# Second block's attention in a two-block network: keys, queries and values reordered, softmax in batches of four heads

## The chip, the cores and the metric

The kernel runs on one core of a Trainium2 chip. The metric is the device time of one execution in microseconds (us). The core has a matrix engine (TensorE, PE in the profile, its weight loads PEld), VectorE (DVE), ScalarE (ACT), GpSimd (POOL), and SyncE (SP), whose queue issues the loads.

## The reference, cut to what matters

256 tokens of width 1024 go through two blocks. The first has a recurrent branch, an attention and a layer of retrieved experts (PEER). The second has two layers; each is a feed-forward half step, a mixer and a second feed-forward half step. The mixer of the second block's first layer is a convolution; that of its second layer is the attention this document is about:

```
k, v = split(rms_norm(x, g_kv) @ w_kv)          # 8 heads of 128
q    = rms_norm(x, g_pre) @ w_q * 128 ** -0.5
s    = q . k - slope[h] * (t_query - t_key)     # causal; slope[h] = 2 ** -(h + 1)
y    = softmax(s) . v
x    = x + rms_norm(y @ w_o, g_post)
```

The keys and values come from one normalisation of x, the queries from another. All 256 tokens lie in one block of the attention, so that no block is left out.

## The kernel before, in words

Products of activations and weights are made in three parts (`mm3`, lines 155 to 159): each operand is split into a high part and the rest, and high x high, high x rest and rest x high are summed in PSUM. Weights come from HBM in units: `Stream.units` (line 115) issues one load of 1 MB into a raw buffer (line 125), ScalarE copies the high part (line 138), VectorE takes the difference (line 141). One load gives two units. In the second block there are three raw buffers and eight buffers for split units (`st.pools`, line 909).

There are two forms of a product. `gemm_rows` (line 230) makes rows of tokens: the tokens' transposed activations are the stationary operand, weights of 512 columns move, and its `tail` says how many of the contraction's chunks are left for tokens 128 to 255 to the end; with `tail=8` all products of tokens 0 to 127 come first, and `late()` makes the others. `gemm_i` (line 216) makes transposed results: the weights are stationary, and the activations of all 256 tokens move at once.

A normalisation is made for 128 tokens at a time. `Pre` (line 950) takes the sum of squares on ScalarE (line 170), the mean on VectorE (line 178), the power on POOL (line 180), scales the rows on VectorE (line 213), transposes them four at a time on TensorE (line 194), copies the high part on ScalarE (line 162) and takes the difference on VectorE (line 163). The feed-forward function `ffn` (line 959) ends with `post(1, ...)` for tokens 128 to 255, and hands the last transpositions on as `pend`, which `run(pend)` at line 1331 issues.

The attention (lines 1335 to 1384) goes in this order:

- values, by `gemm_rows` with `tail=8` (lines 1348 to 1353), evicted by ScalarE into `vr`;
- keys (line 1354), then queries (line 1355), by `gemm_i`, evicted by ScalarE into `kT` and `qT`;
- a loop over eight heads and two halves of the tokens (lines 1359 to 1381): the scores on TensorE (1363), the alibi added (1367) and the maximum (1368) on VectorE, the exponential with its sum on ScalarE (1370), the reciprocal on VectorE (1371), one or two transpositions (1374) with a copy by VectorE (1376), the products with the values (1380), and a scaled eviction by ScalarE (1381);
- the transpositions of the output rows (line 1384), and the output product by `gemm_rows` (line 1385).

Large work tiles of the second block (`Q`, line 918) share five buffers. PSUM has two banks under `pm`, two under `pt` and four under `pa` (line 86).

The engines' queues are not in the written order: the framework's scheduler takes, for each engine, the instruction that comes first in the written order among those that it holds to be ready, with a model of its own for the times. `after` (line 149) adds an order by hand; nothing around the change has one.

Of the kernel before, what the change touches and what calls it, by code (L numbers as in the profile page):

```python
# [9 lines left out]
F32 = mybir.dt.float32  # L10
# [4 lines left out]
AF = mybir.ActivationFunctionType  # L15
ALU = mybir.AluOpType
AX = mybir.AxisListType
# [4 lines left out]
T = 256  # L22
# [44 lines left out]
def _body(nc, tc, ctx, a, out, dbg):  # L67
# [17 lines left out]
    def ps(tag):  # L85
        return pp.tile([128, 512], F32, name=tag, tag=tag, bufs={"pm": 2, "pt": 2, "pa": 4}[tag])
# [173 lines left out]
    def rows_src(w, n):  # L260
        v = w.rearrange("(n c p) d -> n p c d", c=2, p=128)
        return [v[i] for i in range(n)]
# [3 lines left out]

    # ------------------------------------------------------------------ block 1
    with ExitStack() as s1:
# [58 lines left out]

        # recurrent branch input and causal conv
        xp = S([128, 8, TT + 3], F32, "xp")
# [13 lines left out]

        # latent projections
        def small_pair(k, n):
# [56 lines left out]

        # log_sigmoid(lambda) * 8
        lam = pv[:, P_LAM, :]
# [16 lines left out]

        # recurrent gates
        gw, gt = [], []
# [39 lines left out]

        # keys, values, queries
        kT, kodd, vv, qr, qT = [], [], [], [], []
# [88 lines left out]

        # recurrent output
        yT = (S([128, 8, T], F32R, "yTh"), S([128, 8, T], F32R, "yTl"))
# [5 lines left out]

        # attention, with other products between the heads
        mask = tmp("mask", [128, 144 + TT], 1)
# [128 lines left out]

    # ------------------------------------------------------------------ PEER
    with ExitStack() as s2:
# [209 lines left out]

    # ------------------------------------------------------------------ block 2
    with ExitStack() as s3:
# [7 lines left out]
        def t256(name):  # L915
            return bp.tile([128, 256], F32, name=name, tag="t256", bufs=7)
# [158 lines left out]

        # conv mixer
        cv = Q([128, 8, T], F32, "cv")
        # pieces of the convolution: chunk 0 and the first taps of 5 on Pool, two lanes (chunk, first tap, end) on
        # Vector, chunks 6, 7 and the last taps of 5 on PE; a chunk of several pieces is summed by PE, by rows
        VL = (((1, 0, 31), (3, 0, 31)), ((2, 0, 31), (4, 0, 31), (5, KQ, KQ + KS)))  # L1080
# [38 lines left out]
        def taps(lane):  # L1119
            # the sums stay in PSUM: the second read port is left to Pool  # L1120
            bank = ps("pa")
            for j, (b, k0, k1) in enumerate(lane):
                if k0 == k1:
                    return
                dst = t256("part") if k0 else cv[:, b, :]
                parts.setdefault(b, []).append(dst)
                acc = bank[:, j % 2 * T:j % 2 * T + T]
                for k in range(k0, k1):
                    u, o, w = uslot(b)[:, k:k + T], dst if k == k1 - 1 else acc, pv[:, P_DW + k, b:b + 1]
                    if k > k0:  # L1130
                        nc.vector.scalar_tensor_tensor(out=o, in0=u, scalar=w, in1=acc, op0=ALU.mult, op1=ALU.add)
                    elif k == 0:
                        nc.vector.tensor_scalar(o, u, w, pv[:, P_DB, b:b + 1], ALU.mult, ALU.add)
                    else:
                        nc.vector.tensor_scalar(o, u, w, None, ALU.mult)
                    yield

        def taps_pool(b, slot, n):
            # even and odd taps apart, four products at a time
            u = uslot(b)  # L1140
# [51 lines left out]
        def stats(b):  # L1192
            # to rows, as soon as a chunk is done
            n = len(order)
# [26 lines left out]

        # the first chunks by rows, so that the first 128 tokens start before the others are normalized
        wb = {}
# [110 lines left out]

        # block attention
        def G8(n):
# [6 lines left out]
        def ev_copy(dst, scale):  # L1343
            def fn(b, p):
                nc.scalar.activation(dst[:, b, :], p, AF.Copy, scale=scale)
            return fn

        acc, late = gemm_rows(xkv, rows_src(a["wv"], 4), 8)
        for t in range(2):
            for half in range(2):  # L1350
                nc.scalar.activation(vr[:, t, half * 512:half * 512 + 512], acc[t][half], AF.Copy)
            if t == 0:
                late()
        gemm_i([a["wk"][i] for i in range(4)], xkv, ev_copy(kT, 1.0), T)
        gemm_i([a["wq"][i] for i in range(4)], xq, ev_copy(qT, 128.0 ** -0.5), T)
        al = tmp("alibi", [128, 384], 1)
        nc.sync.dma_start(al, a["alibi"])
        orow = Q([128, 2, D], F32, "orow2")
        for h in range(8):
            for t in range(2):  # L1360
                nk = 128 * (t + 1)
                sp = ps("pm")
                nc.tensor.matmul(sp[:, :nk], qT[:, h, t * 128:(t + 1) * 128], kT[:, h, :nk], start=True, stop=True)
                sc = t256("sc2")
                mxv = small.tile([128, 1], F32, name="mxv", tag="mxv", bufs=4)
                av = al[:, 0:128] if t == 0 else al[:, 128:384]
                nc.vector.scalar_tensor_tensor(out=sc[:, :nk], in0=av, scalar=2.0 ** -(h + 1), in1=sp[:, :nk], op0=ALU.mult, op1=ALU.add)
                nc.vector.tensor_reduce(mxv, sc[:, :nk], AX.X, ALU.max, negate=True)
                rsum = small.tile([128, 1], F32, name="rsum", tag="rsum", bufs=4)
                nc.scalar.activation(sc[:, :nk], sc[:, :nk], AF.Exp, bias=mxv, accum_out=rsum)  # L1370
                nc.vector.reciprocal(rsum, rsum)
                pt = ps("pt")
                for j in range(t + 1):
                    nc.tensor.transpose(pt[:, j * 128:(j + 1) * 128], sc[:, j * 128:(j + 1) * 128], ident)
                pT = tmp("pT2", [128, 2, 128], 3)
                nc.vector.tensor_copy(pT[:, :t + 1, :], pt[:, :nk].rearrange("p (j t) -> p j t", j=t + 1))
                po = ps("pa")
                hs = slice(h * 128, h * 128 + 128)
                for j in range(t + 1):
                    nc.tensor.matmul(po[:, :128], pT[:, j, :], vr[:, j, hs], start=j == 0, stop=j == t)  # L1380
                nc.scalar.activation(orow[:, t, hs], po[:, :128], AF.Copy, scale=rsum)
        oT = (q_tile(), q_tile())
        for t in range(2):
            transposes(orow[:, t, :], 8, to_pair(oT[0], oT[1], t * 128, 128))
        acc, late = gemm_rows(oT, rows_src(a["wo"], 4), 8)
        gpost = gain(G_MPOST + 1, bp, bufs=3)
# [101 lines left out]
```

## Time and profile before

| | us |
|---|---|
| median of three runs | 2145.33 |
| lowest and highest | 2144.96, 2150.92 |
| span of the profiled execution | 2144.5 |
| TensorE busy in it | 2093.2 (98%) |
| VectorE, ScalarE, GpSimd busy | 1395.0 (65%), 1143.7 (53%), 113.6 (5%) |

The profile is one execution. A row of the timeline gives the start, the duration, the engine, the line of the code, the operation, output and input tiles, the shape and how many instructions are merged, and in brackets how long the engine had been idle before and for whom it waited. Times are from the start of the span. Matmuls overlap: the record of one lasts longer than the distance to the next start. A row of the windows gives, for a stretch of time, the busy time of each engine with the number of instructions, the granted clock of TensorE (1.00 is full) and the load of the DMA engines.

### The profile page before, as it was taken

To read this page: it belongs to the slowest core of one execution; us is meant where nothing else is said; L and a number is where in the kernel's file an instruction comes from. 1 tells how busy PE (TensorE), PEld (TensorE's weight loads), DVE (VectorE), ACT (ScalarE), POOL (GpSimd) and SP (SyncE) were. 2 spreads that over 40 slices of the span, in tenths; PEclk is the share of its full clock that TensorE was granted. 3 is DMA by queue.
4 is the path that set the end of the run, shared out by engine and by line. 5 is a ranking of instruction groups with operands and counts; after the bars stand their busy time and mean duration, and the time that the engine had idled before them with its cause. 6 is when DMAs were issued, how large, how long until landed. Compare 5 with 4: busy or idle time off the path is not lost.

```text
span 2144.5 us, 31162 instructions
## 1 busy us (share of the span) xinstructions
PE 2093.2 (98%) x12401; PEld 1838.8 (86%) x12401; DVE 1395.0 (65%) x2361; ACT 1143.7 (53%) x1903; POOL 113.6 (5%) x112
## 2 busy tenths in 40 slices
PE   8989999999999999999999999999999999999998
PEld 7889989999999988888887887887887888887886
DVE  6685668888888865555557555967556554756554
ACT  5875444576657744444446444665445444555443
POOL 2010000000000000000000000840000000000000
PEclk9999999999999999999999999999999999999999
DMA  6432554544443445555576554316554654634551
GB/s 212 160 124 96 175 175 163 185 154 159 171 162 137 147 167 191 183 195 184 189 261 230 190 184 170 118 40 248 193 180 170 217 179 157 225 120 165 188 183 72
DMA packets 65361, 365.57 MB, mean 170 GB/s; under 512 B 6704, under 2 KB 8880, under 8 KB 33472
## 3 DMA queue, kind: packets, MB, share of 16 engines
q1 hardware_dynamic: 65216, 363.59, 49.1%
q8 instruction: 97, 1.59, 0.3%
q14 instruction: 48, 0.39, 0.1%
HBM read 360.29 MB, written 2.10 MB: 169 GB/s over the span
## 4 chain that ended last, share of the span: by engine, by line
PE 87%; DVE 5%; ACT 4%; DMA 2%; issue 1%; POOL 1%; SPq 0%; POOLq 0%; DVEq 0%; ACTq 0%
PE pa L157 18%; PE pa L159 18%; PE pa L158 18%; PE pm L157 8%; PE pm L159 8%; PE pm L158 8%; PE pm L801 3%; DVE ws L141 2%; PE pt L194 2%; PE pm L1106 1%; ACT ws L138 1%; DMA raw<-in_ffn_dram 1%; POOL rr L180 1%; ACT sq L170 1%; PE pm L590 1%
## 5 line engine op out<-in xcount | busy, mean ns | idle before, releaser
L141 DVE TENSOR_TENSOR ws<-raw,ws 128x1024 fp32r<-128x1024 f32 (+1 forms) x653 | 795.7, 1225 | 519.8 <-ACT ws L138 514.9
L138 ACT ACTIVATE ws<-raw 128x1024 fp32r<-128x1024 f32 (+1 forms) x657 | 689.3, 1057 | 548.2 <-PE pa L159 347.2
L157 PE MATMUL pa<-xT,ws 128*128 128x256 f32 x1280 | 365.0, 286 | 0.0
L159 PE MATMUL pa<-xT,ws 128*128 128x256 f32 x1280 | 360.9, 282 | 0.0
L158 PE MATMUL pa<-xT,ws 128*128 128x256 f32 x1280 | 360.8, 282 | 0.0
L157 PE MATMUL pm<-ws,xT 128*128 128x512 f32 (+1 forms) x768 | 298.9, 389 | 2.3 <-ACT xT L162 2.3
L159 PE MATMUL pm<-ws,xT 128*128 128x512 f32 (+1 forms) x768 | 294.7, 384 | 2.3 <-DVE xT L163 2.2
L158 PE MATMUL pm<-ws,xT 128*128 128x512 f32 (+1 forms) x768 | 293.8, 383 | 1.1 <-DVE ws L141 1.0
L157 PEld LDWEIGHTS pa<-xT,ws 128*128 128x128 f32 x1280 | 242.1, 189 | 0.3 <-ACT xT L162 0.3
L158 PEld LDWEIGHTS pa<-xT,ws 128*128 128x128 f32 x1280 | 242.0, 189 | 0.0
L159 PEld LDWEIGHTS pa<-xT,ws 128*128 128x128 f32 x1280 | 241.9, 189 | 0.0
L157 PE MATMUL pa<-ws,ch 128*128 128x512 f32 x512 | 201.3, 395 | 1.0 <-ACT ch L162 1.0
L158 PE MATMUL pa<-ws,ch 128*128 128x512 f32 x512 | 201.9, 395 | 0.0
L159 PE MATMUL pa<-ws,ch 128*128 128x512 f32 x512 | 201.5, 394 | 0.0
L159 PEld LDWEIGHTS pm<-ws,xT 128*128 128x128 f32 x768 | 144.8, 189 | 33.0 <-DVE xT L163 3.5
L157 PEld LDWEIGHTS pm<-ws,xT 128*128 128x128 f32 x768 | 144.9, 189 | 30.3 <-ACT xT L162 4.0
L158 PEld LDWEIGHTS pm<-ws,xT 128*128 128x128 f32 x768 | 144.8, 189 | 29.9 <-DVE ws L141 2.5
L157 PE MATMUL pa<-ws,hT 128*128 128x512 f32 x352 | 141.9, 403 | 0.6 <-ACT hT L162 0.5
L159 PE MATMUL pa<-ws,hT 128*128 128x512 f32 x352 | 137.9, 394 | 0.2
L158 PE MATMUL pa<-ws,hT 128*128 128x512 f32 x352 | 137.7, 391 | 0.0
L180 POOL TENSOR_TENSOR rr<-rs,mhalf 128x1 f32<-128x1 f32 (+1 forms) x36 | 28.7, 798 | 1938.9 <-DVE rs L178 1938.9
L157 PEld LDWEIGHTS pa<-ws,ch 128*128 128x128 f32 x512 | 96.4, 188 | 23.6 <-ACT ch L162 1.2
(390 smaller groups left out, 3202.1 us busy)
## 6 DMA issues: line engine op xcount, KB each, us to landing
raw<-in_ffn_dram SPq DMA_DIRECT2D x132, 1024.0 KB, 4.9
raw<-in_peer_u_dram SPq DMA_DIRECT2D x64, 1024.0 KB, 4.9
raw<-in_peer_v_dram SPq DMA_DIRECT2D x64, 1024.0 KB, 4.9
raw<-in_win_dram SPq DMA_DIRECT2D x16, 1024.0 KB, 4.8
gain<-in_gains_dram SPq DMA_DIRECT2D x17, 512.0 KB, 5.6
raw<-in_wpq_dram SPq DMA_DIRECT2D x8, 1024.0 KB, 5.0
raw<-in_wcin_dram SPq DMA_DIRECT2D x8, 1024.0 KB, 4.9
raw<-in_wrnn_dram SPq DMA_DIRECT2D x4, 1024.0 KB, 4.9
```

The lines of the kernel that those rows point to most:

```text
L138: i = nc.scalar.activation(hi, r, AF.Copy)
L141: self.last = (eng or nc.vector).tensor_tensor(out=lo, in0=r, in1=hi.bitcast(F32), op=ALU.subtract)
L157: nc.tensor.matmul(o, wh, xh, start=first, stop=False)
L158: nc.tensor.matmul(o, wh, xl, start=False, stop=False)
L159: nc.tensor.matmul(o, wl, xh, start=False, stop=last)
L170: nc.scalar.activation(sq[:rows, :p.shape[-1]], p, AF.Square, accum_out=ss[:rows, i:i + 1])
L180: nc.gpsimd.tensor_tensor(out=r2[:rows], in0=r[:rows], in1=mhalf[:rows], op=ALU.pow)
L194: nc.tensor.transpose(p[:, j * rows:(j + 1) * rows], src[:rows, (b + j) * 128:(b + j + 1) * 128], ident[:rows, :rows])
L590: nc.tensor.matmul(sp[:, :nk], qT[h // 8][:, h % 8, t * 128:(t + 1) * 128], kT[h // 8][:, h % 8, :nk], start=True, stop=True)
L801: nc.tensor.matmul(p[:, k * 128:(k + 1) * 128], oh[:, k, 0:128], oh[:, k, 128:256], start=True, stop=True)
L1106: in_turn(nc.tensor.matmul(p[:, :T], dg, u[:, k:k + T], start=k == 0, stop=k == 30))
```

## The change

Keys come first, then queries, then values. The softmax is made by batches of four heads and one half of the tokens (`soft2`): scores and alibi are added and the maximum taken by one VectorE instruction, for which the queries of head h are scaled by 2^(h+1) more and the exponential's scale is 2^-(h+1). `flip` transposes the softmax rows of four heads into one PSUM bank and copies the bank at once, by ScalarE for the first half of the keys, by VectorE for the second. `weigh2` makes the products with the values of four heads into one bank and scales them in one VectorE instruction. The first batch's scores come after the second of the four queries products, its transpositions after the third and fourth; the second batch's scores come before the values, its transpositions between the two halves of the values. The transpositions of the output rows of tokens 128 to 255 are written behind the start of the output product. Comments are also taken out elsewhere.

```diff
-        acc, late = gemm_rows(xkv, rows_src(a["wv"], 4), 8)
...
-        gemm_i([a["wk"][i] for i in range(4)], xkv, ev_copy(kT, 1.0), T)
-        gemm_i([a["wq"][i] for i in range(4)], xq, ev_copy(qT, 128.0 ** -0.5), T)
         al = tmp("alibi", [128, 384], 1)
         nc.sync.dma_start(al, a["alibi"])
+        neg = small.tile([128, 8], F32, name="neg")
         for h in range(8):
+            nc.vector.memset(neg[:, h:h + 1], -2.0 ** -(h + 1))
+        pT = {}
...
+        def soft2(g, t):
+            nk = 128 * (t + 1)
+            sc = (tmp("xn", [128, D], 1) if t else tmp("y", [128, 512]))[:, :4 * nk].rearrange("p (h k) -> p h k", h=4)
...
+            for j in range(4):
+                h = 4 * g + j
                 sp = ps("pm")
                 nc.tensor.matmul(sp[:, :nk], qT[:, h, t * 128:(t + 1) * 128], kT[:, h, :nk], start=True, stop=True)
...
+                nc.vector.tensor_tensor_reduce(sc[:, j, :], sp[:, :nk], av, 1.0, -3e38, ALU.add, ALU.max, mxv[:, j:j + 1])
+            nc.vector.tensor_tensor(out=mxv, in0=mxv, in1=neg[:, 4 * g:4 * g + 4], op=ALU.mult)
+            for j in range(4):
+                nc.scalar.activation(sc[:, j, :], sc[:, j, :], AF.Exp, bias=mxv[:, j:j + 1], scale=2.0 ** -(4 * g + j + 1), accum_out=rsum[:, j:j + 1])
+            nc.vector.reciprocal(rsum, rsum)
+            return sc, rsum
+
+        def flip(g, t, sc):
+            if t not in pT:
+                pT[t] = Q([128, 2048], F32, "pT2")
+            v = pT[t][:, g * 512 * (t + 1):(g + 1) * 512 * (t + 1)].rearrange("p (j h q) -> p j h q", j=t + 1, h=4)
+            for j in range(t + 1):
                 pt = ps("pt")
+                for h in range(4):
+                    nc.tensor.transpose(pt[:, h * 128:(h + 1) * 128], sc[:, h, j * 128:(j + 1) * 128], ident)
+                src = pt.rearrange("p (h q) -> p h q", h=4)
+                if j:
+                    nc.vector.tensor_copy(v[:, j], src)
+                else:
+                    nc.scalar.activation(v[:, j], src, AF.Copy)
+            return v
+
+        def weigh2(g, t, v, rsum):
+            po = ps("pm")
+            for h in range(4):
+                hs = slice((4 * g + h) * 128, (4 * g + h + 1) * 128)
                 for j in range(t + 1):
...
+                    nc.tensor.matmul(po[:, h * 128:(h + 1) * 128], v[:, j, h, :], vr[:, j, hs], start=j == 0, stop=j == t)
+            o = orow[:, t, g * 512:(g + 1) * 512].rearrange("p (h w) -> p h w", h=4)
+            nc.vector.tensor_tensor(out=o, in0=po.rearrange("p (h w) -> p h w", h=4), in1=rsum.unsqueeze(2).to_broadcast([128, 4, 128]), op=ALU.mult)
...
+        gemm_i([a["wk"][i] for i in range(4)], xkv, ev_copy(kT, 1.0), T)
+        sm, pv2 = {}, {}
+        for r in range(4):
+            gemm_i([a["wq"][r]], xq, ev_q2(r), T)
+            if r == 1:
+                for t in range(2):
+                    sm[0, t] = soft2(0, t)
+            elif r > 1:
+                pv2[0, r - 2] = flip(0, r - 2, sm[0, r - 2][0])
+        for t in range(2):
+            sm[1, t] = soft2(1, t)
+        acc, late = gemm_rows(xkv, rows_src(a["wv"], 4), 8)
+        for half in range(2):
+            nc.scalar.activation(vr[:, 0, half * 512:half * 512 + 512], acc[0][half], AF.Copy)
+        for t in range(2):
+            pv2[1, t] = flip(1, t, sm[1, t][0])
+        late()
+        orow = Q([128, 2, D], F32, "orow2")
+        for g in range(2):
+            weigh2(g, 0, pv2[g, 0], sm[g, 0][1])
+        for half in range(2):
+            nc.scalar.activation(vr[:, 1, half * 512:half * 512 + 512], acc[1][half], AF.Copy)
         oT = (q_tile(), q_tile())
...
+        for g in range(2):
+            weigh2(g, 1, pv2[g, 1], sm[g, 1][1])
+        otrans2(0)
+        acc, late = gemm_rows(oT, rows_src(a["wo"], 4), 8, fill=(0, lambda: otrans2(1)))
```

## Rows read from the trace of the kernel before

**Rows 1.** The page, part 1: TensorE's busy time, share, instructions.

```profile
PE 2093.2 (98%) x12401; PEld 1838.8 (86%) x12401; DVE 1395.0 (65%) x2361; ACT 1143.7 (53%) x1903; POOL 113.6 (5%) x112
```

**Rows 2.** Windows over the stage that is changed, all engines.

```profile
1831.44:1842.69 11.25, 10.25 (x49) 8.13 (x48) 9.78 (x17) 4.67 (x9) 1.94 (x2) 1.00 0.56 198
1842.69:1857.60 14.91, 14.91 (x72) 12.02 (x73) 8.06 (x11) 8.72 (x12) 0.00 (x0) 1.00 0.39 140
1857.60:1903.35 45.75, 45.75 (x386) 45.74 (x385) 24.01 (x20) 23.99 (x35) 0.00 (x0) 1.00 0.68 240
1903.35:1923.32 19.97, 17.98 (x114) 14.45 (x113) 16.71 (x66) 15.84 (x53) 0.00 (x0) 1.00 0.22 79
```

**Rows 3.** TensorE's timeline at the start of the values' products.

```profile
1831.44 0.39 PE L157 MATMUL pa<-ws,xT 128*128 128x512 f32 x1
1831.67 0.60 PE L194 MATMUL pt<-ident,xn 128*128 128x128 f32 x4
1832.03 0.48 PE L158 MATMUL pa<-ws,xT 128*128 128x512 f32 x1
...
1842.69 0.63 PE L194 MATMUL pt<-ident,xn 128*128 128x128 f32 x4 [1.00 <-DVE xn L213]
```

**Rows 4.** TensorE's timeline in the loop over heads.

```profile
1912.16 0.63 PE L1380 MATMUL pa<-g,pT 128*128 128x128 f32 x4
1912.62 0.38 PE L1374 MATMUL pt<-ident,sc 128*128 128x128 f32 x2
...
1917.15 0.60 PE L1363 MATMUL pm<-g,qT 128*128 128x256 f32 x2
1917.59 0.96 PE L1380 MATMUL pa<-g,pT 128*128 128x128 f32 x6
```

**Rows 5.** ScalarE's timeline while the second half is normalised.

```profile
1831.40 1.06 ACT L138 ACTIVATE ws<-raw 128x1024 fp32r<-128x1024 f32 x1
1832.35 0.60 ACT L170 ACTIVATE sq<-pa 128x512 bf16<-128x512 f32 x1
...
1843.36 1.27 ACT L162 ACTIVATE xT<-pt 128x512 fp32r<-128x512 f32 x2 [3.38 <-PE pt L194]
```

**Rows 6.** VectorE's timeline in the same stretch.

```profile
1834.16 0.15 DVE L173 TENSOR_TENSOR rs<-ss 128x1 f32<-128x1 f32 x1
...
1835.60 0.14 DVE L178 TENSOR_SCALAR rs<-rs 128x1 f32<-128x1 f32 x1
...
1838.65 2.35 DVE L141 TENSOR_TENSOR ws<-raw,ws 128x1024 fp32r<-128x1024 f32 x2
1840.92 0.15 DVE L178 TENSOR_SCALAR rs<-ss 128x1 f32<-128x1 f32 x1
...
1843.99 0.69 DVE L163 TENSOR_TENSOR xT<-pt,xT 128x512 fp32r<-128x512 f32 x1 [0.78 <-ACT xT L162]
```

**Rows 7.** Windows between block 1 and PEER, TensorE alone.

```profile
287.46:290.98 3.52, 0.01 (x1) 1.00 0.96 301
...
292.29:295.95 3.66, 3.66 (x18) 0.53 0.17 55
295.95:302.00 6.05, 6.05 (x52) 1.00 0.24 58
```

**Rows 8.** Windows at the convolution's end, TensorE alone.

```profile
1419.25:1422.80 3.55, 2.81 (x13) 0.50 0.66 270
1422.80:1425.52 2.72, 2.72 (x8) 0.50 0.00 0
```

**Rows 9.** Window over block 1's attention, all engines.

```profile
135.00:208.00 73.00, 73.00 (x565) 68.53 (x564) 41.16 (x120) 41.91 (x109) 0.00 (x0) 1.00 0.34 116
```

**Rows 10.** Groups by line and shape, 1900 to 1926: busy time, mean ns.

```profile
L1367 DVE SCALAR_TENSOR_TENSOR sc<-alibi,pm 128x256 f32<-128x256 f32 x8 | 3.3, 413 | 0.0
```

**Rows 11.** Groups by line and shape, 135 to 208, block 1's attention.

```profile
L591 DVE CUSTOM_DVE_ANT_0 sc<-pm,mask 128x272 f32<-128x272 f32 x16 | 7.0, 439 | 2.1 <-PE pm L590 1.8
```

**Rows 12.** Instructions of the alibi tile: durations, first and last start.

```profile
L1357 SPq DMA_DIRECT2D alibi<-in_alibi_dram x1: 425/425/425, 1118.9 to 1118.9; - x1
```

## What was predicted before the change was run

> **What bounds the kernel now.** I read the page first, then the windows over the stage that is changed, then TensorE's timeline at both ends of it, and last the timelines of ScalarE and VectorE. The page says that TensorE is busy for 98% of the span [rows 1], so only two things can move the time: TensorE's work, which the change leaves nearly as it is, and the moments in which TensorE has nothing to do. The windows [rows 2] cut the stage in four: the values while the second half of the tokens is still being normalised (1831.44 to 1842.69), the rest of the values (to 1857.60), keys and queries (to 1903.35), the loop over heads (to 1923.32, where the output products start). Keys and queries run without a gap. The other stretches hold all that an order of work can win or lose, so I price these.
>
> Prices of TensorE's work, from one start to the next. Keys and queries: 384 products in 45.75 us [rows 2] (the row counts two that reach in), 0.119 us each. Four transpositions take 0.36 us (1831.67 to 1832.03) [rows 3], 0.09 each. In the loop, four instructions of the product with the values take 0.46 us (1912.16 to 1912.62) and two 256-wide score instructions 0.44 us (1917.15 to 1917.59) [rows 4], so 0.115 and 0.22; a 128-wide score instruction I set at 0.115 too. A 512-wide product takes 0.23 us (1831.44 to 1831.67) [rows 3]; the values have 96 of them, 22.1 us.
>
> **Idle time in the start, before.** From 1831.44 to 1857.60 there are 26.2 us. 22.1 are the values, 2.2 are six groups of four transpositions, so 1.9 us are lost. What the reader is to see: the feed-forward stage is over at 1831.44, where the first of the values' products starts, and the transpositions of the second half's normalised tokens start only at 1842.69 [rows 3]. These 11 us are covered by the values' products for tokens 0 to 127, which need the first half alone: TensorE is busy for 10.25 of 11.25 us [rows 2].
>
> **Idle time in the loop, before.** 1903.35 to 1923.32 is 19.97 us, and two of the four groups of output transpositions come after it. Work: scores 16 x 0.115 + 16 x 0.22 = 5.4, softmax transpositions 24 x 0.09 = 2.2, products with the values 48 x 0.115 = 5.5, eight output transpositions 0.7: 13.8 us. So 6.2 us are lost there, in many small steps, because TensorE has no other products between a head's softmax steps. The busy column shows only 2.0 us of idleness (19.97 less 17.98), since a matmul's record lasts longer than the distance to the next start.
> The Trainium skill says (Perfetto Trace Analysis, Identifying the Most-Contended Engine) that matmul busy time is a poor measure, and points to the weight loads instead. By it the sum below would use 19.97 less 14.45 = 5.5 us in place of 6.2, and come to 2153.3 us; by the busy column 2.0, and 2156.8 us. The trace agrees with the rule: starts give 6.2.
>
> **The change, part by part.**
> *1. Keys first (a loss).* The keys' products are 256 wide: each takes both halves of the tokens at once. So none can start before the second half is normalised, transposed and split. I assume that the chain up to there keeps its times, because all of it, and the work that it waits behind on ScalarE and VectorE, comes before the change. The second half's transpositions then start at 1842.69; ScalarE's copy follows at 1843.36 [rows 5], VectorE's difference at 1843.99 and lasts 0.69 us [rows 6]; the keys' second product needs it, so the keys run from 1844.7. From 1831.44 that is 13.3 us, in which TensorE has four groups of transpositions (1.4 us): 11.9 us lost in place of 1.9, a loss of **10.0 us**. Lower end: the chain loses time behind other work. The second square waited behind a weight copy (1831.40 to 1832.35) [rows 5]; the scaling at 1835.60 came 1.3 us after its sum; the one at 1840.92 came after a pair of weight differences that began at 1838.65 [rows 6]. Without these some 4 us go, and the loss is 6. Upper end: 11, if the second differences come later still.
> *2. The clock (a loss).* After a hole of 3.52 us, where PEER's first products wait for block 1, the granted clock was 0.53 over 3.66 us: 18 products there against 52 in the next 6.05 us [rows 7], so 3.66 - 18 x 0.116 = 1.6 us lost, at the lower of the two levels (1.2 GHz, where 2.4 is full). In the convolution the clock stood at 0.50 over 3.55 + 2.72 us [rows 8], half of which, 3.1 us, is lost at most. Here the hole is about 9 us, longer than the first, and work resumes with transpositions as in the second, part of the low stretch passing before the keys start. I take **2.0**, ends 0.3 and 3.1.
> The Trainium skill (TensorE: Matmul & The Clock Gate, Why this matters for your kernels) advises against idle gaps between bursts, since the clock falls in them. That speaks against putting the keys first; the two stretches above agree with it.
> *3. Scores and softmax under other products (a gain).* The scores of heads 0 to 3 come after the second queries product, those of 4 to 7 ahead of the values; transpositions lie under queries and values. Block 1 does its attention so, and TensorE is busy there for 73.00 of 73.00 us [rows 9]. What stays uncovered is the end: the last values eviction, the normalised rows, ScalarE's copy of 0.6 and VectorE's 0.69 before the output products can take the first half. I leave **1.5 us** of the 6.2 there; ends 0 (block 1's row) and 6.2 (nothing won). Gain 4.7.
> *4. VectorE and ScalarE, at nothing.* The sum of score and alibi, 0.41 us for 256 columns [rows 10], and the maximum behind it become one instruction, of which block 1 shows 0.44 for 272 columns [rows 11]. Sixteen copies of softmax rows become two of 512 on VectorE and four on ScalarE, sixteen scaled evictions become four on VectorE. Both engines get less to do, and the cover is wide: over keys and queries each is busy for 24.0 of 45.75 us [rows 2]. If the cover went, one batch would show, four of 0.44 = 1.8 us on VectorE and about as much again on ScalarE. Eight memsets and the four-column multiplications are tiny and free to run early.
> *5. The queues.* SP's loads of 1 MB each are the same twelve in another order: the keys' take the place of the values' first four, loaded during the feed-forward stage. The values' units must be kept until their late half, so the output weights are split only while the last products run; this costs nothing if VectorE keeps the 1.2 us a unit of the pair at 1838.65, up to 1.5 us if not (in the ends of 3). The alibi load was issued at 1118.9 [rows 12], 780 us ahead of its use, and stays early. POOL's queue holds nothing that moves.
> *6. Buffers.* The new transposed softmax needs two of five large buffers; both halves' normalised tokens (four) and the queries hold all five until the queries are done. So the first batch's transpositions wait for the last queries product, and the second batch's scores of tokens 128 to 255 wait for them (they share the row buffer). That falls under the values' first half, 11 us of products: nothing. If it does not fit, up to 4 us.
>
> **Sum.** +10.0 + 2.0 - 4.7 = +7.3 us. The profiled execution's span is 2144.5 us, 0.8 under the median of 2145.33 and 0.5 under the lowest run, so span and what lies around it fit the median: 2145.3 + 7.3 = **2152.6 us**, slower by 0.34%. About 0.3%, 6.4 us, is what a measurement of this kernel tells from no change, so faster means under 2138.9 and slower over 2151.7.
>
> **Rivals.**
> *A cheap hole.* The order of each queue is chosen by a scheduler, as the alibi load shows; with the same hole the chain might run without the work that it waited behind: loss 6, clock 1.5, gain 4.7, so +2.8: 2148.1, no change that can be told. For it: each delay named in 1 is other engines' filling. Against it: that filling is older than the change.
> *The hole is filled (not slower).* If the scheduler pulled up the values' first-half products, which need only what is there at 1831.44, the loss of 1 and 2 vanishes: -4.7, 2140.6, no change; with the 1.9 us and all 6.2 won, 2137.2, faster. Decisive is whether values' weights can be split before the keys'. Against it: there are eight split buffers, given in the order of the loads, and the keys' eight units take them all until the keys' products release them.
> *A worse end (slower).* Loss 11, clock 3.1, and of the 6.2 nothing won for the buffers of 6 and the late output weights of 5: +14, 2159. For it: the five large buffers are full. Against it: the values' cover of 11 us.
> That the order of the products comes out as before, so that the change does not do what it says, I give no chance of its own: written order sets who gets the weight buffers.
>
> **How the numbers follow.** Forecast 0.55, its own range 2149 to 2156, of which 0.40 lies above 2151.7 and 0.15 below; cheap hole 0.22; filled 0.10, of which 0.04 faster; worse end 0.13. Slower 0.40 + 0.13 = 0.53, same 0.15 + 0.22 + 0.06 = 0.43, faster 0.04. The range takes in the cheap hole with a margin below and the worse end above, 2146 to 2159; outside stay the filled hole and a rest, under 0.2.
>
> **What would show it.** Right: in the changed profile TensorE idles some 9 us between the feed-forward's last product and the second half's transpositions, the granted clock is about 0.5 for the first microseconds of the keys, and from the last values product to the first output product there lie some 8 us, not 20. Wrong, step 1: products with the values stand in that gap, or the second half's transpositions come within 8 us. Step 2: clock 1.00 there. Step 3: gaps above 1 us between queries, values and output.

## The result, and the profile after

The change took 2162.34 us (median of four runs, 2161.08 to 2162.72), the kernel before beside it 2145.91 (four runs, 2144.96 to 2150.92): a ratio of 1.0068, 95% interval 1.0056 to 1.008. It is slower, as forecast, but by 16.4 us in place of 7.3, and above the range.

First the page of the kernel after, its span and part 1 (busy time, share and instructions of each engine).

```profile
span 2160.8 us, 31113 instructions
PE 2101.2 (97%) x12401; PEld 1843.4 (85%) x12401; DVE 1393.8 (65%) x2351; ACT 1143.1 (53%) x1891; POOL 113.1 (5%) x112
```

TensorE does the same 12401 products as in [rows 1] and the span is 16.3 us longer. Next the TensorE timeline after, at both ends of the changed stage; it answers to [rows 3] and [rows 4].

```profile
1838.36 0.39 PE L159 MATMUL pa<-ws,hT 128*128 128x512 f32 x1
1838.67 0.66 PE L194 MATMUL pt<-ident,xn 128*128 128x128 f32 x4
1840.03 0.63 PE L194 MATMUL pt<-ident,xn 128*128 128x128 f32 x4 [0.70 <-DVE xT L163]
1849.84 1.94 PE L194 MATMUL pt<-ident,xn 128*128 128x128 f32 x8 [9.18 <-DVE xn L213]
1851.62 1.01 PE L157 MATMUL pa<-xT,ws 128*128 128x256 f32 x3
...
1930.33 0.39 PE L159 MATMUL pa<-ws,xT 128*128 128x512 f32 x1
1930.56 1.95 PE L1399 MATMUL pm<-g,pT 128*128 128x128 f32 x16
1933.41 3.84 PE L1399 MATMUL pm<-g,pT 128*128 128x128 f32 x32 [0.91 <-DVE orow L1401]
1937.09 1.04 PE L194 MATMUL pt<-ident,orow 128*128 128x128 f32 x8
1938.38 0.50 PE L157 MATMUL pa<-ws,xT 128*128 128x512 f32 x1 [0.25 <-ACT xT L162]
```

The forecast's picture is all there: the hole of 9.18 us, then the keys; at the end products with the values without a break between them but one of 0.91 us, and 8 us from the last values product to the first output product. The windows after answer to [rows 2]: chain up to the second half's transpositions, first keys, keys and queries, values, end.

```profile
1838.35:1849.84 11.49, 1.61 (x10) 0.87 (x9) 10.02 (x17) 4.91 (x9) 1.94 (x2) 0.72 0.61 206
1849.84:1857.81 7.97, 7.97 (x52) 7.72 (x53) 4.54 (x8) 3.45 (x5) 0.00 (x0) 0.77 0.69 252
1857.81:1906.74 48.93, 48.91 (x394) 47.70 (x393) 24.21 (x46) 26.76 (x50) 0.00 (x0) 1.00 0.44 151
1906.74:1930.56 23.82, 23.75 (x110) 19.16 (x109) 6.35 (x17) 11.19 (x26) 0.00 (x0) 1.00 0.16 46
1930.56:1938.38 7.82, 6.66 (x58) 6.23 (x56) 7.49 (x9) 4.41 (x7) 0.00 (x0) 1.00 0.96 347
```

But the same last feed-forward product that started at 1831.21 before starts at 1838.36. I cut the span at two products that both kernels have: that one, and the first product of the last feed-forward stage, behind the attention. First the two in the kernel before, then the second of them after:

```profile
1831.21 0.40 PE L159 MATMUL pa<-ws,hT 128*128 128x512 f32 x1
1947.89 0.50 PE L157 MATMUL pm<-ws,xT 128*128 128x512 f32 x1 [0.45 <-ACT xT L162]
```

```profile
1963.30 0.50 PE L157 MATMUL pm<-ws,xT 128*128 128x512 f32 x1 [0.45 <-ACT xT L162]
```

Each column is a start in the trace, or a difference of two starts, or of a start and the span's end.

```
                         up to the stage   the stage   behind it    span
before                       1831.21         116.68      196.62    2144.5
after                        1838.36         124.94      197.46    2160.8
difference                     +7.15          +8.26       +0.85     +16.3
```

So in these two executions the changed stage costs 8.3 us, and 8.0 us come from stages whose code the change doesn't touch. The trace by tile shows such a stretch: the 88 transpositions of `hh`, in the two feed-forward stages that lie ahead of the attention, first before, then after (durations in ns, then first and last start).

```profile
L194 PE MATMUL pt<-ident,hh x88: 270/271/329, 1463.4 to 1825.9; 128*128 128x128 f32 x88
```

```profile
L194 PE MATMUL pt<-ident,hh x88: 270/272/328, 1467.9 to 1833.1; 128*128 128x128 f32 x88
```

From the first start to the last the same work takes 362.5 us before and 365.2 after, and 4.5 us were lost before it began. There is no gap that grew in this stretch, and its granted clock is 1.00 in both kernels. The page's busy time of TensorE grows too, by 8.0 us for the same 12401 products.

### The profile page after: what moved, and what is told of

It is laid out like the page before. It is cut to its first block, busy times and chain, and to the rows that moved or that the text cites. A ratio compares the mean times of both kernels' runs of the same rounds, so it can differ in the third digit from the quotient of the medians.

```text
span 2160.8 us, 31113 instructions
## 1 busy us (share of the span) xinstructions
PE 2101.2 (97%) x12401; PEld 1843.4 (85%) x12401; DVE 1393.8 (65%) x2351; ACT 1143.1 (53%) x1891; POOL 113.1 (5%) x112
## 4 chain that ended last, share of the span: by engine, by line
PE 87%; DVE 7%; ACT 3%; issue 1%; POOL 1%; DMA 1%; SPq 0%; POOLq 0%; DVEq 0%; ACTq 0%
PE pa L157 19%; PE pa L159 19%; PE pa L158 19%; PE pm L157 8%; PE pm L159 8%; PE pm L158 8%; PE pm L801 3%; DVE ws L141 2%; DVE pa L1131 2%; PE pt L194 2%; ACT ws L138 1%; POOL rr L180 1%; ACT sq L170 1%; PE pm L590 1%; PE pa L622 1%
```

## The experiments

**What the theories were.** The only thing that the change puts ahead of the stage is the tile `neg` with its eight memsets, which run 0.9 to 1.1 us after the start. It is given 32 bytes of each partition in the pool `small`, so all tiles of the later pools lie 32 bytes higher, while the first pool's tiles (`xT`, some of the raw and split weights) stay where they were (addresses of the built programs). Theory: that place costs the 8 us, and the stage itself behaves as forecast. Rivals: the memsets, or another order that they bring into the queues; or the new attention itself, by its loads and buffers.

**e1_pad32: the kernel before, with the tile and the memsets alone.**

```diff
         al = tmp("alibi", [128, 384], 1)
         nc.sync.dma_start(al, a["alibi"])
+        neg = small.tile([128, 8], F32, name="neg")
+        for h in range(8):
+            nc.vector.memset(neg[:, h:h + 1], -2.0 ** -(h + 1))
```

> The kernel before with one thing of the change alone: the 32-byte tile of slopes, in the pool that lies ahead of all later pools in SBUF, and its eight memsets; nothing reads it. Theory of the place: every tile of the later pools lies 32 bytes higher, and the same instructions in the same order run slower, 7 us up to the attention and 1 us behind it: 2153 to 2155 us. Rival, that the 7 us ahead of the attention belong to one execution or to the changed stage in some other way: 2145 to 2147 us.

Measured: 2153.42 us beside 2145.63, ratio 1.0031 (1.0019 to 1.0043), 7.8 us between the medians, 6.7 by the ratio, for a tile that nothing reads. The `hh` row of this kernel, 365.1 us from first to last start:

```profile
L194 PE MATMUL pt<-ident,hh x88: 270/272/328, 1467.6 to 1832.7; 128*128 128x128 f32 x88
```

**e2_pad64 and e9_pad96: the same with 64 and 96 bytes.**

```diff
-        neg = small.tile([128, 8], F32, name="neg")
+        neg = small.tile([128, 16], F32, name="neg")
```

> The same with a tile of 64 bytes. If a shift by a multiple of 64 bytes puts the tiles back into the same position against the memory's own rows, 2145 to 2147 us, as before; if any shift costs, or the memsets do, 2153 to 2155 us. By the rival again 2145 to 2147 us.

> The kernel before with the unused tile of slopes at 96 bytes, one and a half rows of 64. If the position within 64 bytes against the first pool decides, as 32 bytes: 2152 to 2155 us. If it was the 32 bytes for a reason of their own, 2145 to 2148 us.

Measured: 64 bytes 2147.72 us, ratio 1.001 (1.0001 to 1.0019); 96 bytes 2152.09, ratio 1.0026 (1.0016 to 1.0036). The eight memsets are in both, so they aren't the cost. The `hh` rows, 64 bytes (362.8 us) and then 96 (365.0):

```profile
L194 PE MATMUL pt<-ident,hh x88: 270/272/328, 1463.3 to 1826.1; 128*128 128x128 f32 x88
```

```profile
L194 PE MATMUL pt<-ident,hh x88: 270/271/329, 1466.0 to 1831.0; 128*128 128x128 f32 x88
```

**e5_all32: 32 bytes ahead of every pool.**

```diff
     gp = pool(ctx, "glob")
+    lead = gp.tile([128, 8], F32, name="lead")
+    nc.vector.memset(lead, 0.0)
```

> The kernel before with 32 bytes of nothing ahead of every other tile, so that all tiles lie 32 bytes higher, the first pool's (activations, two raw and three split weight buffers) with the rest. If it counts where a tile lies in the memory's own rows of 64 bytes, all are now in the worse position: 2153 us or more. If it counts how the first pool's tiles lie against the later pools', nothing has changed between them: 2145 to 2148 us.

Measured: 2146.68 us beside 2146.43, ratio 1.0004 (0.9995 to 1.0013), and 362.7 us in the `hh` row (two lines of code lie ahead, so L194 is L196 here):

```profile
L196 PE MATMUL pt<-ident,hh x88: 270/272/328, 1463.0 to 1825.7; 128*128 128x128 f32 x88
```

In the traces of these four kernels every engine has the same instructions in the same order as before, apart from the memsets, so another order in the queues isn't the cause either. Where the later pools lie is all the same as long as the first pool moves with them. What costs is a distance of 32 or 96 bytes between pools more than before; 64 costs little. In the built programs the activations and split weights of the second block start 32 bytes past a multiple of 64 in the kernel before and in e2; in e1 and e9 those in the later pool start at a multiple, in e5 all do. So what the slow kernels share is that the two pools stand differently within 64 bytes; that the memory itself has rows of 64 bytes, as the expectations put it, is a theory that no run shows.

The stages that the change doesn't touch, by the first transposition of `hh` and the two cuts of the table above (us):

```
                      first hh    from it to the stage    behind the stage
before                 1145.63           685.58                196.62
e5, 32 B ahead of all  1145.47           685.49                196.62
e2, 64 B               1146.29           685.07                195.71
e3, below              1145.56           685.89                196.56
after                  1147.07           691.29                197.46
e1, 32 B               1146.76           691.25                197.44
e9, 96 B               1144.84           691.48                197.35
```

With the shift the two stretches take 5.7 to 5.9 and 0.7 to 0.9 us more than before, some 6.6 in all, in each of three kernels; the five kernels below that aren't listed here have 685.3 to 685.8 and 196.5 to 196.7. The first column doesn't follow the shift: e9 begins first, and e10, without it, last of all, at 1147.29. So 1.4 of the 8.0 us are no more than executions differ by.

Which products grow? I took the distance of each start to the next of the 512-wide three-part products from 1440 to 1830 us (distances under 0.26 us), grouped by the pools of the two operands; means in ns, and the count before.

```
stationary, moving           before     32 B     96 B     64 B    count
xT first, ws later           229.22   233.45   234.08   232.42     325
xT2 later, ws first          229.59   233.33   233.37   227.96     169
hT0 later, ws first          229.83   233.29   233.05   229.04     124
hT1 later, ws first          230.22   232.91   232.92   229.61      59
xT2 later, ws later          228.13   227.88   227.61   227.48     341
xT first, ws first           232.53   232.54   232.85   232.63     204
```

The products with operands in different pools became slower by 2.7 to 4.9 ns; those with both in one pool (hT0 and hT1 with later weights too, which aren't listed) changed by less than 1. With e5's common shift all pairs stay within 0.3 ns of the kernel before. At 32 bytes the increases times the counts are 1.4 + 0.6 + 0.4 + 0.2 = 2.6 us, which is the 2.6 by which the `hh` row grew. Two rows don't fit a rule by the place within 64 bytes alone: with 64 bytes, xT with later weights is slow all the same, and the pair within the first pool has 232.5 to 232.9 in every kernel. What in the memory makes the difference is not shown.

Some 1.5 us come by another way, once: in the convolution the granted clock falls. Windows of TensorE before, then after, then in e1_pad32:

```profile
1361.00:1366.00 5.00, 5.00 (x44) 1.00 0.17 68
```

```profile
1361.00:1366.00 5.00, 5.00 (x31) 0.66 0.50 201
```

```profile
1361.00:1366.00 5.00, 5.00 (x32) 0.66 0.49 193
```

About 3.4 us run at the lower level (1.2 GHz of 2.4), where 16 products start 0.21 us apart and not 0.12. In e9 the same happens 2 us earlier. The other nine kernels stay at 1.00. The wait ahead of it doesn't tell them apart; this is its end before and after:

```profile
1358.67 0.38 PE L157 MATMUL pt<-xT,ws 128*128 128x256 f32 x1 [2.16 <-DVE ud L1167]
```

```profile
1360.74 0.39 PE L157 MATMUL pt<-xT,ws 128*128 128x256 f32 x1 [2.13 <-DVE ud L1167]
```

It lasts 2.11 to 2.17 us in all twelve kernels. Why the clock falls behind it only in the three with the shift is not shown.

**e3_change_unshifted: the whole change, with the tile in the second block's own pool, behind the others, where it moves nothing else.**

```diff
-        neg = small.tile([128, 8], F32, name="neg")
+        neg = tmp("neg", [128, 8], 1)
```

> The whole change, with the tile of slopes moved into the second block's own pool, behind everything else, so that no other tile's address differs from the kernel before. Theory of the place: only the stage is left, +8 us by the shift between the two profiles from 1831 to 1925: 2153 to 2155 us. Rival: as the change, 2161 to 2163 us.

Measured: 2154.29 us, ratio 1.0038 (1.0024 to 1.0052). By the medians 8.05 us of the change's time are gone by this one line, and what is left, 8.7 over 2145.63, is near the forecast's 7.3 and inside its range. The `hh` stretch is back at 362.6 us (1463.6 to 1826.2). The windows of TensorE in this kernel, cut at the end of the hole and at the end of the low clock:

```profile
1831.76:1843.30 11.54, 1.66 (x11) 0.66 0.62 202
1843.30:1849.10 5.80, 5.80 (x28) 0.51 0.77 305
1849.10:1852.00 2.90, 2.90 (x27) 1.00 0.10 34
```

28 instructions at 0.51 in 5.80 us, then 27 in 2.90: half speed. The low stretch begins inside the hole, which has 0.66 on the whole, and outlasts it. In [rows 7] the hole itself stood at 1.00 and the low stretch came behind it.

**e4_order_only: keys, queries, values; the loop over heads as before, no `neg`.**

```diff
+        gemm_i([a["wk"][i] for i in range(4)], xkv, ev_copy(kT, 1.0), T)
+        gemm_i([a["wq"][i] for i in range(4)], xq, ev_copy(qT, 128.0 ** -0.5), T)
         acc, late = gemm_rows(xkv, rows_src(a["wv"], 4), 8)
...
-        gemm_i([a["wk"][i] for i in range(4)], xkv, ev_copy(kT, 1.0), T)
-        gemm_i([a["wq"][i] for i in range(4)], xq, ev_copy(qT, 128.0 ** -0.5), T)
```

> Keys, queries, values in this order, with the old loop over heads behind them: the loss of the order without the gain of the batches. Theory (hole of 9 to 10 us and half a clock for some microseconds behind it): +11 to +13, 2157 to 2159 us. Rival, that the hole costs less and the batches won nothing: 2153 to 2155 us.

Measured: 2158.66 us, ratio 1.0051 (1.0037 to 1.0065); the stage of its profile takes 128.77, 12.1 us more than before. Parts 1 and 2 of the forecast are 10.0 + 2.0; less a clock of 1.5 to 2.5 (e7, below) the stage leaves 9.6 to 10.6 for the hole. The timeline of TensorE in this kernel shows the hole at the same place:

```profile
1831.95 0.40 PE L159 MATMUL pa<-ws,hT 128*128 128x512 f32 x1
1832.26 0.66 PE L194 MATMUL pt<-ident,xn 128*128 128x128 f32 x4
1833.61 0.63 PE L194 MATMUL pt<-ident,xn 128*128 128x128 f32 x4 [0.70 <-DVE xT L163]
1843.43 1.94 PE L194 MATMUL pt<-ident,xn 128*128 128x128 f32 x8 [9.18 <-DVE xn L213]
1845.20 1.01 PE L157 MATMUL pa<-xT,ws 128*128 128x256 f32 x3
```

**e6_batches_only: values first as before, then keys, and the change's batches of four heads under the queries; tile as in e3.** The edit is against the kernel after.

```diff
+        acc, late = gemm_rows(xkv, rows_src(a["wv"], 4), 8)
...
         gemm_i([a["wk"][i] for i in range(4)], xkv, ev_copy(kT, 1.0), T)
         sm, pv2 = {}, {}
...
-        acc, late = gemm_rows(xkv, rows_src(a["wv"], 4), 8)
```

> The batches without the new order: values, keys, queries as before, then the softmax of heads 0 to 3 under the third and fourth queries products, that of heads 4 to 7 behind the queries with nothing to cover it but the other batch's products with the values; the slopes unshifted. Theory (the batches won 4.4 us in the change, where both were covered, here one is): 2141 to 2144 us. Rival, that the gain came from the cover of the values alone: 2146 us or more.

Measured: 2143.19 us beside 2146.43, ratio 0.9985 (0.9976 to 0.9994), stage 114.40, 2.3 us less than before. So the batches gain without the new order, though the last one has no products above it. From e4 to e3 they gain 2.8 us by the stages of one profile each (128.77 to 125.99) and 4.4 by the medians, but e4's runs spread from 2155.05 to 2159.59.

**e7_warm: e3 with 36 products of the first half's tokens written ahead of the keys; their result is read by nothing.**

```diff
+        idle = ps("pm")
+        for i in range(36):
+            nc.tensor.matmul(idle, xkv[0][:, i % 8, 0:128], xkv[0][:, 0:4, 0:128], start=True, stop=True)
         gemm_i([a["wk"][i] for i in range(4)], xkv, ev_copy(kT, 1.0), T)
```

> The change unshifted, with 36 products of 512 columns into a bank that nothing reads, of the first half's tokens alone, written ahead of the keys: they fill the hole of 9 us and change nothing else. Theory: the granted clock stays at 1.00 when the keys begin, and the time falls by what the low clock cost, 1.5 to 2.5 us below the unshifted change (2154.3): 2152 to 2153 us. Rival, that the clock cost nothing because the chain and not TensorE's rate sets the start of the stage: no difference, 2154 us.

Measured: 2152.75 us, ratio 1.0031 (1.0018 to 1.0043), stage 123.48. Timeline and windows of TensorE in this kernel:

```profile
1832.86 7.30 PE L1408 MATMUL pm<-xT 128*128 128x512 f32 x31
1842.14 1.29 PE L194 MATMUL pt<-ident,xn 128*128 128x128 f32 x8 [1.98 <-DVE xn L213]
```

```profile
1830.36:1841.00 10.64, 9.80 (x48) 1.00 0.61 223
1841.00:1846.00 5.00, 3.80 (x27) 1.00 0.86 299
1846.00:1850.00 4.00, 4.00 (x36) 1.00 0.46 161
```

With the hole full of useless products the clock stays at 1.00 and the stage is 2.5 us shorter than e3's, 1.5 shorter than the change's own (whose low clock ended earlier behind the hole, at 1853.3, 1.7 us after the keys began). That is the clock's price, 1.5 by the medians too; the rest of the loss is that the products come late. The Trainium skill (TensorE: Matmul & The Clock Gate, Why this matters for your kernels) advises against idle gaps between bursts; the trace agrees, 0.51 after a hole of 9.18 us and 1.00 after one of 1.98.

**e10_chain_free: e3, with VectorE's differences for the second to fourth load of the keys' weights ordered behind the second half's row scaling.**

```diff
-            nc.vector.scalar_tensor_tensor(out=xn[:rows, s], in0=src[:, s], ...
+            norm_only.last = nc.vector.scalar_tensor_tensor(out=xn[:rows, s], in0=src[:, s], ...
...
+        gemm_i([a["wk"][0]], xkv, ev_copy(kT, 1.0), T)
+        st.behind = norm_only.last
+        for r in range(1, 4):
+            gemm_i([a["wk"][r]], xkv, lambda ob, p, r=r: ev_copy(kT, 1.0)(2 * r + ob, p), T)
+        st.behind = None
```

> The change unshifted, with VectorE's weight differences of the second to fourth keys loads ordered behind the second half's last scaling of rows, so that none of them runs inside the chain of the normalisation. Theory (0.9 us of the hole is VectorE's pair ahead of the mean, 0.8 us the power on POOL, which takes 1.39 us beside a difference and 0.55 us alone): 1.5 to 2 us less than the unshifted change's 2154.3, 2152 to 2153 us. Rival of the cheap hole, 4 us less: 2150 us.

Measured: 2152.68 us, ratio 1.0029 (1.0018 to 1.004), 1.6 under e3. POOL's two powers in e3, then here (lines are three further on), then TensorE's hole here:

```profile
1836.12 1.40 POOL L180 TENSOR_TENSOR rr<-rs,mhalf 128x1 f32<-128x1 f32 x1 [9.81 <-DVE rs L178]
1841.44 0.55 POOL L180 TENSOR_TENSOR rr<-rs,mhalf 128x1 f32<-128x1 f32 x1 [3.92 <-DVE rs L178]
```

```profile
1835.84 0.55 POOL L183 TENSOR_TENSOR rr<-rs,mhalf 128x1 f32<-128x1 f32 x1 [9.20 <-DVE rs L181]
1839.62 0.55 POOL L183 TENSOR_TENSOR rr<-rs,mhalf 128x1 f32<-128x1 f32 x1 [3.23 <-DVE rs L181]
```

```profile
1841.10 1.94 PE L197 MATMUL pt<-ident,xn 128*128 128x128 f32 x8 [6.55 <-DVE xn L216]
```

The second half's transpositions come 1.8 us earlier (1842.92 in e3), in an execution that reached the chain's first square 0.8 us later (1831.38 against 1830.58); the hole is 2.6 us shorter, 6.55 in place of 9.18. The medians show 1.6 of it, or 2.5 if each kernel is set against the runs of the kernel before beside it. So VectorE's weight differences do hold the chain up, but the rival "a cheap hole" wanted 4 us of it, and got some 2, and only with an order written by hand.

**e8_pairs: values, keys, queries; batches of two heads, each scored behind its own queries product and transposed under the next; tile as in e3.** The edit is against the kernel after; the lines that cut the batches to two heads are left out.

```diff
+        acc, late = gemm_rows(xkv, rows_src(a["wv"], 4), 8)
...
         for r in range(4):
             gemm_i([a["wq"][r]], xq, ev_q2(r), T)
+            for t in range(2):
+                if r:
+                    pv2[r - 1, t] = flip(r - 1, t, sm[r - 1, t][0])
+            for t in range(2):
+                sm[r, t] = soft2(r, t)
```

> Values, keys, queries as before, and the softmax in batches of two heads, each behind its own queries product, so that only the last two heads' softmax has no queries products over it; the slopes unshifted. Theory (no hole, three of four batches covered): 2139 to 2142 us, below the kernel before and below the batches of four. Rival, that the smaller batches give back in evictions and waits what the cover wins: 2143 to 2146 us.

Measured: 2140.24 us (ten runs, 2139.39 to 2142.23) beside 2146.43, ratio 0.9974 (0.9965 to 0.9983), stage 111.65, 5.0 us less than before. TensorE's timeline from the last queries product to the first output product:

```profile
1909.15 0.28 PE L159 MATMUL pa<-xT,ws 128*128 128x256 f32 x1
1909.28 0.38 PE L1388 MATMUL pt<-ident,sc 128*128 128x128 f32 x2
...
1910.38 0.83 PE L1401 MATMUL pa<-g,pT 128*128 128x128 f32 x6
1911.08 1.13 PE L1371 MATMUL pm<-g,qT 128*128 128x256 f32 x4
1912.05 3.51 PE L1401 MATMUL pa<-g,pT 128*128 128x128 f32 x30
...
1918.49 0.47 PE L157 MATMUL pa<-ws,xT 128*128 128x512 f32 x1
```

9.2 us from 1909.28 to 1918.49, where [rows 2] had 19.97 from 1903.35 on. Three of the four batches have their softmax done when the queries' products end, and the last one's lies under the products of those three with the values, which are all there by then. This version keeps the cover at the start and wins the end, and beats both kernels, the one before by 0.26%.

## Why the prediction was wrong, and where it was right

**The step that failed is part 4, the terms at nothing,** in the words "Eight memsets and the four-column multiplications are tiny and free to run early". That is so for the instructions: the memsets take 59 ns each, and e2 has all eight of them and takes 2.1 us more. But the tile that they write was given no price. By its place ahead of the later pools it cost 7.8 us alone (e1) and 8.05 in the change (after less e3) by the medians, 6.6 by what three traces repeat. With it fell the premise under part 1 that what "comes before the change" keeps its times: 7.15 of the 16.3 us lie ahead of the stage, of which 1.4 fall before 1147 us, where kernels without the shift differ as much, and 0.85 behind. Neither the range nor a rival had room for a cost in other stages; no row of the profile before could have given its size, yet the diff shows a new tile in a pool that lies ahead of others.

**Part 1, the hole: right.** From the last feed-forward product to the second half's transpositions the trace has 11.48 us before and after, and from it to the first keys product 13.26 (the forecast has 13.3, from a start 0.23 us later). Order alone cost 12.1 us by the stage, 13.0 by the medians, where parts 1 and 2 say 12.0. The scheduler moved nothing into the hole, so that rival fell, and e10 puts the cheap hole at 2.6 us by the trace, 1.6 by the medians, in place of 4.

**Part 2, the clock: right.** 1.5 us in the change's profile and 2.5 in e3's, against 2.0 (e7).

**Part 3, the batches: the mechanism is right, the size by the profiles some 1.5 to 2 us too large.** The end is as forecast: 7.82 us from the first product with the values to the first output product, of which 48 x 0.115 and 8 x 0.09 are work, leaves 1.6 us, where 1.5 was said. But the stage gained 2.8 (e4 to e3), not 4.7; the medians of the two have 4.4, so the size stays uncertain. The cover isn't free: in e7, at full clock, the 384 keys and queries products take 47.2 us from start to start, 1.5 more than the 45.74 before. Seven of them, next to scores or to the softmax's transpositions, have 0.20 to 0.31 us to the next start and not 0.12, 1.0 us in all; the rest lies at the normalisation's transpositions, which were under the values before.

**Parts 5 and 6: nothing, right.** The second batch's scores and transpositions lie under the values, the first batch's first transpositions came even before the last queries product (1896.63, that product 1902.70), and of the waits at the end only 0.91 us for VectorE's scaled rows and 0.25 for ScalarE's copy are left.

Together, from the profiles: 10.0 + 1.5 - 3.2 = 8.3 us for the stage. The 10.0 is the forecast's own term, which e4 bears out; the 3.2 is what e7, which has no low clock, leaves of it (123.48 - 116.68 = 6.8). Forecast were 7.3. With the 8.0 outside it this is the 16.3. The direction came out right for the reasons given, for e3 without the shift is slower too; the size did not, for one reason that the forecast never looked at.

## What to carry to other kernels

Before a change is costed at nothing outside its stage, look at which tiles it adds and what lies behind them in memory: a small new tile early in the pools moves everything after it, and each product whose operands come from both sides of it can change its time. Put small new tiles behind all others, and compare a stage that the change doesn't touch first. In the stage itself: batching a softmax under other products and reordering those products were two edits, one worth 2 to 6 us and the other costing 12; the cover at the start of a stage is as valuable as that at its end.

## What the runs showed of the hardware that was not expected

- 32 bytes per partition between two pools made 512-wide products with one operand in each slower by 2.7 to 4.2 ns of 230, and the kernel by 0.31%; 96 bytes cost 0.26%, 64 bytes 0.1% with an interval that just leaves out zero, and 32 bytes under all pools nothing that could be measured. A window that is full in both kernels doesn't show it; the starts do, and the page's busy time for the same products (2093.2 us before, 2101.0 in e1). No run tells what in the memory does it, nor why the clock fell in the convolution with it.
- POOL's power of one column takes 1.40 us beside a VectorE difference and 0.55 alone (e3 and e10; 1.39 and 0.55 in the kernel before). The Trainium skill (GPSIMD Engine Reference, Specifications) says that GpSimd shares its memory interfaces with VectorE and contends with instructions there that read two inputs from that memory; the trace agrees, the difference reading `raw` and `ws`; beside the difference at line 163, which reads one of its two inputs from PSUM, e10's first power takes 0.55 all the same.
